# Zeros on TensorE inside the scans, the second expert's list on VectorE, and an early Silu table

## The chip, the cores and the metric

The kernel runs on one core of a Trainium2 chip. The time is device microseconds of that core, for the whole layer, all inputs in DRAM at the start and the output in DRAM at the end. The core has a matrix engine (TensorE, "PE" in the profile, with its weight loads as "PEld"), VectorE ("DVE"), ScalarE ("ACT"), GpSimd ("POOL") and SyncE ("SP", which issues most DMAs here). Lower is better.

## The reference

One encoder layer on 512 tokens of 1024 features, in float32. A mixer (eight heads of a chunked state-space scan beside eight heads of attention with a forget gate) is followed by a layer norm; then a mixture of 16 experts, top 2 of one group of four, and a second layer norm:

```
proj = x @ w_in + b_in                  # z, xBC, dt, q, k, v, f
xbc  = silu(causal_conv(xBC));  y = ssd_scan(...) * silu(z), group RMS norm
att  = forgetting_attention(q, k, v, log_sigmoid(f))
h    = layer_norm(alpha * x + concat(y, att) @ w_out)
...
g_idx = top1(softmax(h @ rg_w + rg_b));  e_val, e_idx = top2(softmax(h @ re_w[g_idx] + re_b))
for e in range(16):
    act = silu(h @ w_gate[e]) * (h @ w_up[e])
    out = out + combine[:, e:e+1] * (act @ w_down[e])
return layer_norm(alpha * h + out)
```

## The kernel before, in words

Products are made of two halves: each float32 operand is split into a rounded part (made by ScalarE) and a remainder (made by VectorE or GpSimd), and three products hi*hi, hi*lo, lo*hi are added in PSUM. `split` and `wsplit` make such pairs.

The first half of the kernel is the mixer. Two generators are woven into TensorE's stream: `prep(g)` makes the projections, convolutions and row forms of one scan group (g = 0, 1), and `scan(g)` runs the four chunks of its scan. `fill_stream` supplies further projections between the steps. In `prep`, `x_rows(c)` transposes chunk c of the two convolved tiles `x2[0]`, `x2[1]` into a PSUM bank `pxt`, which VectorE reads into xd and xsd. In `scan`, `decay(c)` makes the decay logits `pl` (a bank with the tag "s") and then the products of B and C in `pcb`. `pxt`, `pcb`, `pms` and others share two PSUM banks with the tag "t": a new tile waits until the last reader of the one that held its bank has finished. TensorE's order is written by hand throughout (`MANUAL`); the order of VectorE, ScalarE, GpSimd and SyncE is made by a planner with its own costs, except inside `tc.manual_schedule(engines=VECTOR)`, where the order in the code holds for VectorE, ScalarE and GpSimd. Instructions that come later in the code and outside may still be placed between these.

Such a hand-ordered section stands between the mixer and the experts (lines 1334 to 1403). It makes the output projection, the first layer norm and the routing by blocks of 128 tokens: `choose` ranks, `seat` numbers each expert's tokens in `place`, `weigh` makes the weights (`r1` is the exponential of the second choice's logit). The first expert's tokens are collected specially: a gather for two blocks, and for the other two a product with one-hot matrices (`picks`, `px_add`) into the banks `px`. `split` turns px into `xgh` and `xgl`, the first expert's input.

Each other expert needs a list. `seats_of` compares `seats` (1 to 128 along a row) with a token's place and makes four one-hot matrices of 128x128, on the engine that it is given; `list_of` multiplies them on TensorE with `entry` (token number and weight), and VectorE makes the index `ix` and the weight `wc`; `gather` fetches the rows of `hb` (the layer norm's result in DRAM) by an indirect DMA of GpSimd. `call(e)` is all three. The expert loop (from line 1418) runs for expert e: `gate_up` in four steps; after three (`EARLY`) `call(e + 2)`; Silu and the multiplication; `xg_T` transposes the next expert's rows; `act_T` transposes the activations; `down` multiplies by w_down, one expert later. The second expert's `call(1, False)` stands after the first step of the first expert; `weights_of_first` makes the lists' weights for the first three experts inside the second expert.

Memory on the chip is given out by tags: "u" (weights and larger tiles) and "q" (small ones, 6 buffers, among them the one-hot matrices and the activations).

Of the kernel before, what the change touches and what calls it, by code (L numbers as in the profile page):

```python
# [9 lines left out]
BF16 = mybir.dt.bfloat16  # L10
# [6 lines left out]
P = 128  # L17
# [52 lines left out]
def hybrid_layer(ctx: ExitStack, tc: tile.TileContext, x, xT, wu, w16, bT, bz, bv, b16, cw, cb,  # L70
# [15 lines left out]
    def bank(tag, name):  # L86
        return ps.tile([P, 512], F32, tag=tag, name=name)
# [65 lines left out]
    def Q(name, dt=F32):  # L153
        return slab.tile([P, 256], dt, tag="q", name=name, bufs=NQ)
# [3 lines left out]
        return t_[:, :512], t_[:, 512:]  # L158


    idle = Q("idle", BF16)[:, :P]
    V.memset(idle, 0.0)
    cx = big.enter_context(tc.tile_pool(name="cx", bufs=1))
    ph1 = ExitStack()
    sm = ph1.enter_context(tc.tile_pool(name="sm", bufs=1))
# [287 lines left out]
    def prep(g):  # L453

        w = G_[g]
        u0 = 6 + 3 * g
        hs = slice(4 * g, 4 * g + 4)
        if g:
            load_unit(u0)
        r = []  # L460
        if g:
            yield from proj_T(u0, 0, r)
            load_unit(u0 + 1)
        else:
            yield from proj_T2(u0, r)
            r = [conv_in(pt, m) for m, pt in ((1, r[0]), (0, r[1]))]
            done.add("u6")
            yield 0.0
        b2 = conv2(r.pop() if g == 0 else conv_in(r.pop(), 4 * g), 4 * g)
        w["bh"], w["bl"] = halves("b")  # L470
        split_half(w["bh"], w["bl"], b2)
        if g:
            yield from proj_T(u0, 1, r)
        c2 = conv2(r.pop() if g == 0 else conv_in(r.pop(), 4 * g + 1), 4 * g + 1)
        w["ch"], w["cl"] = halves("c")
        split_half(w["ch"], w["cl"], c2)
        yield from proj_T(u0 + 1, 0, r)
        load_unit(u0 + 2)
        if g == 0:
            SY.dma_start(bz_sb, bcast_rows(bz, 512))  # L480
            SY.dma_start(g_sb, bcast_rows(ssd_g, 512))
        x2 = [conv2(conv_in(r.pop(), 4 * g + 2), 4 * g + 2)]
        pbt = bank("t", "pbt")
        for c in range(3):
            T.transpose(pbt[:, c * P:(c + 1) * P], b2[:, c * P:(c + 1) * P], identf)
        yield 0.32
        w["bth"], w["btl"] = halves("bt")
        split_half(w["bth"][:, :3 * P], w["btl"][:, :3 * P], pbt[:, :3 * P])
        yield from proj_T(u0 + 1, 1, r)
        x2.append(conv2(conv_in(r.pop(), 4 * g + 3), 4 * g + 3))  # L490
        xeh, xel = (rows4(U(n, F32R)) for n in ("xeh", "xel"))

        xd2 = [U("xd2", F32R).rearrange("p (t g d) -> p t g d", t=2, g=2) for _ in range(2)]
        xdp = [xd2[c // 2][:, c % 2] for c in range(NT)]
        xsd = rows4(U("xsd"))
        zs = rows4(U("zs"))
        w.update(xdp=xdp, xeh=xeh, xel=xel, xsd=xsd, zs=zs)

        def x_rows(c):
            pxt = bank("t", "pxt")[:, :256]  # L500
            for m in range(2):
                T.transpose(pxt[:, m * P:(m + 1) * P], x2[m][:, c * P:(c + 1) * P], identf)
            xd = Q("xd")
            tt4(xd, pxt, dth[:, c, hs], OP.mult)
            A.activation(xdp[c][:, 0], xd, AF.Copy)
            if c < 3:
                xe = Q("xe")
                tt4(xe, xd, dec[:, c, hs], OP.mult)
                A.activation(xeh[:, c], xe, AF.Copy)
            tt4(xsd[:, c], pxt, dsh[:, hs], OP.mult)  # L510
            V.tensor_tensor(xdp[c][:, 1], xd, xdp[c][:, 0].bitcast(F32), op=OP.subtract)
            if c < 3:
                V.tensor_tensor(xel[:, c], xe, xeh[:, c].bitcast(F32), op=OP.subtract)

        for t in range(NT):
            yield from proj_R(u0 + 2, t, r)
            zf = Q("zf")
            V.tensor_tensor(zf, r.pop(), bz_sb[:, g * 256:(g + 1) * 256], op=OP.add)
            th = Q("zth")
            A.activation(th, zf, AF.Tanh, scale=0.5)  # L520
            V.scalar_tensor_tensor(zs[:, t], th, 1.0, zf, op0=OP.add, op1=OP.mult)
            if t >= XLAG[g]:
                x_rows(t - XLAG[g])
                yield 0.22
        for t in range(NT - XLAG[g], NT):
            x_rows(t)
            yield 0.22

    def scan(g):
# [9 lines left out]
        def decay(c):  # L539

            cs = slice(c * P, (c + 1) * P)
            pl = bank("s", "pl")
            for i in range(2):
                T.matmul(pl, lhsT=csel[:, c], rhs=RL[g][i], start=(i == 0), stop=False)
            T.matmul(pl, lhsT=identb, rhs=maskl[:, None, :].to_broadcast([P, 4, P]), start=False, stop=True)
            pcb = bank("t", "pcb")[:, :P]
            for i, (b_, c_) in enumerate((("bh", "ch"), ("bh", "cl"), ("bl", "ch"))):
                T.matmul(pcb, lhsT=w[b_][:, cs], rhs=w[c_][:, cs], start=(i == 0), stop=(i == 2))
            lt = U("lt")[:, :512].rearrange("p (h l) -> p h l", l=P)
            V.tensor_tensor(lt, pl.rearrange("p (h l) -> p h l", l=P),  # L550
                            ac3[:, c, hs][:, :, None].to_broadcast([P, 4, P]), op=OP.subtract)
            A.activation(lt, lt, AF.Exp)
            V.tensor_tensor(lt, lt, pcb[:, None, :].to_broadcast([P, 4, P]), op=OP.mult)
            mt[c] = [h_.rearrange("p (h l) -> p h l", l=P) for h_ in halves("mt")]
            split(*mt[c], lt)
# [321 lines left out]
    if MANUAL:  # L877
        ctx.enter_context(tc.manual_schedule(engines=MANUAL))
    g_sb, bz_sb = halves("g_bz", F32)
    pt = bank("t", "idle")  # L880
    for _ in range(10):
        T.matmul(pt, lhsT=idle, rhs=idle[:, None, :].to_broadcast([P, 4, P]), start=True, stop=True)
    first = prep(0)
    until("u6", first)
    weave(gates(), f=first)
# [79 lines left out]
    def entry_of(e):  # L965
        return lambda t: entry[:, t, EO[e]]

    def call(e, weights=True):
        se = seats_of(lp, lambda t: place[:, t, EO[e]:EO[e] + 1], G)
        ix, wc = list_of(lp, se, entry_of(e), weights=weights)  # L970
        gather(ix, xgs[e % 2])
        lists[e] = [ix, wc if weights else se]
# [325 lines left out]
    def weigh():  # L1298
# [8 lines left out]
        for k in (1, 0):  # L1307
            V.scalar_tensor_tensor(oh[k], CH["rank"][:, :, 1:5], float(k), og, op0=OP.is_equal, op1=OP.mult)
            if k:
                t_ = R([4, 4], "t_")  # L1310
                V.tensor_tensor(t_, oh[k], lg4[:, :, 1:5], op=OP.mult)
                oh0, oh1 = (o_.rearrange("p t g e -> p t (g e)") for o_ in oh)
                V.tensor_reduce(r1, t_.rearrange("p t g e -> p t (g e)"), axis=AX.X, op=OP.add)
                A.activation(r1, r1, AF.Exp)
        yield
        V.tensor_reduce(gs, gx, axis=AX.X, op=OP.add)
        V.scalar_tensor_tensor(gs, r1, 1.0, gs, op0=OP.add, op1=OP.mult)
# [16 lines left out]
    with tc.manual_schedule(engines=VECTOR):  # L1334
# [54 lines left out]
            picks(t)  # L1389
        norm_bias(3)  # L1390
        norm_store(3, hb, G)
        px_add(hh[2], pick[2], range(KC))
        dsp[0, 2] = wsplit(raw[0, 2])
        wg = weigh()
# [2 lines left out]
        for hf in range(2):  # L1397
            px_add(hh[3], pick[3], range(4 * hf, 4 * hf + 4), True)
            split(*(t_[:, hf * 4:hf * 4 + 4] for t_ in xt_), px[hf].rearrange("p (k s) -> p k s", s=P))
        for t in range(2, 4):  # L1400
            norm_store(t, ub, G)
        load_pieces(NPRE, NPRE + GATED, G)
# [1 line left out]

    def weights_of_first():

        lists[0] = list_of(lp, seats_of(lp, lambda t: place[:, t, EO[0]:EO[0] + 1], G), entry_of(0))
        for e in (1, 2):
            lists[e][1] = list_of(lp, lists[e][1], entry_of(e), tokens=False)[1]

        pn = bank("s", "pcnt")[:, :16]
        for tt in range(NT):
            T.matmul(pn, lhsT=onesb, rhs=mskb[:, tt], start=(tt == 0), stop=(tt == NT - 1))
        V.tensor_reduce(cnt_i, pn, axis=AX.X, op=OP.max)
        rt.close()

    at = {}
    for e in range(NEXP - 2):
        load_pieces(NPRE + 12 * e + (0 if e else GATED), NPRE + 12 + 12 * e)
        gu = gate_up(e, xt_, "pj" if e else "o")  # L1420
        for n in range(EARLY):
            next(gu)
            if e == 0 and n == 0:
                call(1, False)
        call(e + 2, bool(e))
        if e == 0:
            drop(wg)
        if e == 1:
            weights_of_first()
        drop(gu)  # L1430
        xt_ = xg_T(xgs[(e + 1) % 2])
        for d in DOWN[e]:
            def between(f):
                if f == ACT_AT and d != e and e in DOWN[e]:
                    at[e] = act_T(e)
            finish(d, down(d, at.pop(d), between=between))
        if e not in DOWN[e]:
            at[e] = act_T(e)
# [182 lines left out]
```

## Time and profile before

| | us |
|---|---|
| median of 3 runs (lowest, highest) | 629.06 (626.08, 634.25) |
| profiled execution, its own time | 632.85 |
| its span, first to last instruction | 631.1 |
| TensorE busy | 578.6 (92%) |
| VectorE busy | 526.4 (83%) |
| ScalarE busy | 409.7 (65%) |
| GpSimd busy | 195.8 (31%) |
| mean granted clock of TensorE | 0.973 |

Times in the profile are microseconds from the span's start. "PEclk" is the clock that TensorE was granted, as a share of 2.4 GHz. Line numbers are those of the kernel before.

### The profile page before, as it was taken

The page shows a single profiled execution, that of the slowest core. Times are in us where ns is not written, and L with a number is a line of the kernel's source. Part 1 is how long each engine was busy: PE and PEld are TensorE (multiplying, and loading weights), DVE is VectorE, ACT ScalarE, POOL GpSimd, SP SyncE. Part 2 cuts the span into 40 slices and gives each one's busy share as a digit, 9 for nine tenths or more (in the row PEclk, how much of TensorE's full clock was granted, in tenths as well). Part 3 has the DMA queues.
Part 4 walks back from the last instruction along what each step waited for, and adds up shares of the span by engine and source line. Part 5 has one row for each costly group of instructions (what it writes and reads, how often), then busy time and mean ns, then how long its engine had stood idle before and what let it go on. Part 6 is the DMA issues. An engine that isn't in the chain of part 4 may idle for free.

```text
span 631.1 us, 9108 instructions
## 1 busy us (share of the span) xinstructions
PE 578.6 (92%) x3020; PEld 472.7 (75%) x3021; DVE 526.4 (83%) x904; ACT 409.7 (65%) x640; POOL 195.8 (31%) x221
## 2 busy tenths in 40 slices
PE   6997997899999989999789999999999999999790
PEld 4786887788777758778667888888888888877550
DVE  3897598888668787668778999999999999999883
ACT  5575363543577776422267888888888888888660
POOL 6300000033553441014472223433343233412341
PEclk9998898999999999999889999999999999999996
DMA  8621021221222174994799999999999999998531
GB/s 264 209 68 60 8 77 59 84 68 65 70 68 66 36 238 133 389 344 175 281 389 319 304 382 344 386 361 358 355 346 342 328 352 373 346 339 287 190 122 61
DMA packets 62102, 142.73 MB, mean 226 GB/s; under 512 B 10073, under 2 KB 10073, under 8 KB 62048
## 3 DMA queue, kind: packets, MB, share of 16 engines
q1 hardware_dynamic: 55712, 127.88, 56.4%
q0 software_dynamic: 6336, 14.20, 7.6%
q8 instruction: 25, 0.41, 0.3%
q14 instruction: 29, 0.24, 0.1%
HBM read 136.26 MB, written 14.68 MB: 239 GB/s over the span
## 4 chain that ended last, share of the span: by engine, by line
PE 52%; DVE 16%; DMA 16%; issue 7%; ACT 6%; POOL 2%; POOLq 0%; SPq 0%; ACTq 0%; DVEq 0%
DMA xg<-ub,ix 6%; PE pw L807 4%; PE pg L1004 4%; PE pg L1006 4%; PE pg L1005 4%; PE pjT L241 4%; PE pu L1004 4%; PE pu L1006 4%; PE pu L1005 4%; PE py L1043 3%; PE py L1041 3%; PE py L1042 3%; DMA ub<-yo,ix 3%; PE pjR L265 3%; DMA xg<-hb,ix 2%
## 5 line engine op out<-in xcount | busy, mean ns | idle before, releaser
L987 ACT ACTIVATE eh<-wf 128x1024 fp32r<-128x1024 f32 x188 | 198.7, 1060 | 49.6 <-PE pg L1006 16.4
L1004 PE MATMUL pg<-eh,xgh 128*128 128x512 f32 x128 | 53.3, 416 | 0.8 <-ACT xgh L90 0.8
L958 POOL DMA_INDIRECT xg<-hb,ix x16 | 21.5, 1343 | 99.9 <-PE pg L1006 77.6
L1006 PE MATMUL pg<-eh,xgl 128*128 128x512 f32 x128 | 50.2, 393 | 1.3 <-DVE xgl L91 1.3
L1049 POOL DMA_INDIRECT ub<-yo,ix x14 | 27.2, 1945 | 74.5 <-ACT at L90 57.7
L937 POOL TENSOR_SCALAR se<-seats,place 128x128 bf16<-128x128 f32 x64 | 49.5, 784 | 1.6 <-PE pat L1022 1.1
L1004 PE MATMUL pu<-eh,xgh 128*128 128x512 f32 x128 | 49.9, 390 | 0.0
L1006 PE MATMUL pu<-eh,xgl 128*128 128x512 f32 x128 | 49.8, 389 | 0.0
L1041 PE MATMUL py<-eh,at 128*128 128x512 f32 x120 | 48.5, 404 | 1.0 <-ACT at L90 0.7
L241 PE MATMUL pjT<-xh,wh 128*128 128x512 f32 x112 | 47.6, 425 | 1.6 <-DVE kl L671 1.6
L1043 PE MATMUL py<-eh,at 128*128 128x512 f32 x120 | 47.1, 392 | 0.0
L241 PE MATMUL pjT<-xh,wl 128*128 128x512 f32 x112 | 45.0, 402 | 0.0
L241 PE MATMUL pjT<-xl,wh 128*128 128x512 f32 x112 | 45.0, 402 | 0.0
L265 PE MATMUL pjR<-wh,xh 128*128 128x256 f32 x128 | 38.6, 302 | 1.2 <-DVE vf L643 1.2
L265 PE MATMUL pjR<-wl,xh 128*128 128x256 f32 x128 | 37.5, 293 | 0.0
L265 PE MATMUL pjR<-wh,xl 128*128 128x256 f32 x128 | 37.4, 292 | 0.0
L130 POOL TENSOR_TENSOR rst<-rst,mhalf 128x1 f32<-128x1 f32 x8 | 4.6, 578 | 100.5 <-DVE rst L129 100.5
L1006 PEld LDWEIGHTS pg<-eh,xgl 128*128 128x128 f32 x128 | 24.1, 188 | 7.4 <-DVE xgl L91 2.2
L225 POOL TENSOR_TENSOR wl<-wr,wh 128x512 fp32r<-128x512 f32 x16 | 21.4, 1362 | 25.9 <-ACT wh L220 25.9
L1004 PEld LDWEIGHTS pg<-eh,xgh 128*128 128x128 f32 x128 | 24.2, 189 | 5.3 <-ACT xgh L90 1.2
L220 ACT ACTIVATE wh<-wr 128x1024 fp32r<-128x1024 f32 x22 | 23.1, 1054 | 7.5 <-PE pjT L241 3.4
L1006 PEld LDWEIGHTS pu<-eh,xgl 128*128 128x128 f32 x128 | 24.0, 188 | 5.1
(971 smaller groups left out, 1756.4 us busy)
## 6 DMA issues: line engine op xcount, KB each, us to landing
wf<-in_w_up SPq DMA_DIRECT2D x64, 512.0 KB
wf<-in_w_gate SPq DMA_DIRECT2D x64, 512.0 KB
wf<-in_w_down SPq DMA_DIRECT2D x62, 512.0 KB
wr<-in_wu SPq DMA_DIRECT2D x22, 512.0 KB
wor<-in_w_out SPq DMA_DIRECT2D x8, 512.0 KB
hh<-in_x SPq DMA_DIRECT2D x4, 512.0 KB
hb<-hh POOLq DMA_DIRECT2D x4, 512.0 KB, 4.8
ub<-hh POOLq DMA_DIRECT2D x4, 512.0 KB, 5.6
```

What stands on the lines that cost most here:

```text
L220: A.activation(h_, wr_, AF.Copy)
L241: T.matmul(pt, lhsT=w_[:, k % 4, m * P:(m + 1) * P], rhs=x_[k], start=(i == 0), stop=(i == 23))
L265: T.matmul(pt, lhsT=x_[k][:, t * P:(t + 1) * P], rhs=w_[:, k % 4, :], start=(i == 0), stop=(i == 23))
L807: T.matmul(pw, lhsT=m_[k][:, ts_], rhs=wo[k][w_][:, c_], start=(i == 0), stop=(i == 11))
L937: eng.tensor_scalar(r[t], seats, place_(t), None, op0=OP.is_equal)
L987: A.activation(h_, src, AF.Copy)
L1004: T.matmul(pt, lhsT=h_[:, k], rhs=wh_[:, f], start=(k == 0), stop=False)
L1005: T.matmul(pt, lhsT=h_[:, k], rhs=wl_[:, f], start=False, stop=False)
L1006: T.matmul(pt, lhsT=l_[:, k], rhs=wh_[:, f], start=False, stop=(k == KC - 1))
L1041: T.matmul(pt, lhsT=h_[:, f], rhs=wh_[:, c_], start=(f == 0), stop=False)
L1043: T.matmul(pt, lhsT=l_[:, f], rhs=wh_[:, c_], start=False, stop=(f == 3 and rows is None))
L1049: G.indirect_dma_start(out=ub, out_offset=bass.IndirectOffsetOnAxis(ap=ix, axis=0), in_=yo, in_offset=None, bounds_check=S - 1, oob_is_err ...
```

## The change

There are three groups of edits. (1) The ten products of zeros at the start become a function `idle(pt, n)`, which multiplies zeros (a tile of one column, read 128 and 512 times) into a PSUM bank. It is called with 6 ahead of the transposes of `x_rows(0)`, in both groups, and with 7 ahead of `pcb` of the first chunk of the first group. (2) The second expert's matrices are made by VectorE in the hand-ordered section, right after the last block's layer norm has been stored, and its list and gather follow the splits of the first expert's input, ahead of that expert's products. The first expert's own matrices (for its weights) are made one expert earlier, and its list is made last in `weights_of_first`. (3) A Silu of `r1`, whose result nobody reads, follows the exponential of `r1` on ScalarE.

```diff
-    idle = Q("idle", BF16)[:, :P]
-    V.memset(idle, 0.0)
+    zeros = const.tile([P, 1], BF16, name="zeros")
+    V.memset(zeros, 0.0)
+
+    def idle(pt, n):
+
+        for _ in range(n):
+            nc.tensor.matmul(pt, lhsT=zeros.to_broadcast([P, P]), rhs=zeros.to_broadcast([P, 512]), start=True, stop=True)
...
         def x_rows(c):
-            pxt = bank("t", "pxt")[:, :256]
+            pxt = bank("t", "pxt")
+            if c == 0:
+                idle(pxt, 6)
+            pxt = pxt[:, :256]
...
-            pcb = bank("t", "pcb")[:, :P]
+            pcb = bank("t", "pcb")
+            if c == 0 and g == 0:
+                idle(pcb, 7)
+            pcb = pcb[:, :P]
...
-    pt = bank("t", "idle")
-    for _ in range(10):
-        T.matmul(pt, lhsT=idle, rhs=idle[:, None, :].to_broadcast([P, 4, P]), start=True, stop=True)
+    idle(bank("t", "idle"), 10)
...
-    def call(e, weights=True):
-        se = seats_of(lp, lambda t: place[:, t, EO[e]:EO[e] + 1], G)
+    def call(e, weights=True, se=None):
+        se = se or seats_of(lp, lambda t: place[:, t, EO[e]:EO[e] + 1], G)
...
                 A.activation(r1, r1, AF.Exp)
+
+                A.activation(R([], "tab"), r1, AF.Silu)
...
         norm_store(3, hb, G)
+        se1 = seats_of(lp, lambda t: place[:, t, EO[1]:EO[1] + 1], V)
         px_add(hh[2], pick[2], range(KC))
...
             split(*(t_[:, hf * 4:hf * 4 + 4] for t_ in xt_), px[hf].rearrange("p (k s) -> p k s", s=P))
+        call(1, False, se1)
         for t in range(2, 4):
             norm_store(t, ub, G)
...
-        lists[0] = list_of(lp, seats_of(lp, lambda t: place[:, t, EO[0]:EO[0] + 1], G), entry_of(0))
         for e in (1, 2):
             lists[e][1] = list_of(lp, lists[e][1], entry_of(e), tokens=False)[1]
+        lists[0] = list_of(lp, lists[0], entry_of(0))
...
-        for n in range(EARLY):
+        for _ in range(EARLY):
             next(gu)
-            if e == 0 and n == 0:
-                call(1, False)
         call(e + 2, bool(e))
         if e == 0:
             drop(wg)
+            lists[0] = seats_of(lp, lambda t: place[:, t, EO[0]:EO[0] + 1], G)
```

## Rows read from the trace of the kernel before

**Rows 1.** Stretches: busy time of each engine, granted clock, DMA share, GB/s.
```profile
core 0: us, PE busy (x) PEld busy (x) DVE busy (x) ACT busy (x) POOL busy (x), PEclk, DMA share, GB/s
6.40:9.30 2.90, 2.90 (x14) 2.21 (x12) 0.69 (x1) 1.26 (x2) 0.69 (x1) 1.00 0.99 328
...
50.30:53.70 3.40, 3.40 (x19) 3.40 (x18) 2.43 (x7) 1.22 (x4) 0.00 (x0) 0.51 0.03 5
...
61.05:67.40 6.35, 6.35 (x17) 5.09 (x18) 3.83 (x9) 2.09 (x4) 0.00 (x0) 0.50 0.27 82
...
104.90:108.30 3.40, 3.40 (x18) 3.40 (x18) 2.90 (x8) 0.00 (x0) 0.33 (x1) 0.51 0.00 0
...
196.00:200.00 4.00, 2.44 (x13) 1.59 (x11) 3.96 (x10) 1.66 (x6) 2.52 (x4) 1.00 0.37 131
...
313.10:324.10 11.00, 10.99 (x54) 8.59 (x54) 10.57 (x19) 8.31 (x10) 7.63 (x9) 1.00 1.03 382
...
327.10:330.20 3.10, 3.09 (x14) 3.00 (x15) 1.15 (x2) 1.68 (x3) 2.01 (x5) 0.50 1.04 394
...
384.00:400.00 16.00, 16.00 (x81) 13.15 (x80) 15.33 (x20) 13.74 (x17) 5.86 (x6) 1.00 1.00 345
```

**Rows 2.** Timeline of TensorE in the mixer: start, duration, line, operation, [idle before <-releaser].
```profile
2.87 3.85 PE L882 MATMUL idle<-idle 128*128 128x512 bf16 x10 [2.87 <-DVE idle L162]
...
47.24 0.27 PE L502 MATMUL pxt<-identf,acc 128*128 128x128 f32 x1
49.39 0.33 PE L502 MATMUL pxt<-identf,acc 128*128 128x128 f32 x1 [1.88 <-DVE acc L436]
...
61.05 0.87 PE L548 MATMUL pcb<-c,b 128*128 128x128 f32 x3 [2.73 <-DVE xsd L445]
...
104.44 0.33 PE L502 MATMUL pxt<-identf,acc 128*128 128x128 f32 x1 [2.31 <-DVE rst L129]
...
198.29 0.50 PE L723 MATMUL po<-pl,v 128*128 128x512 f32 x1 [1.56 <-DVE pl L91]
```

**Rows 3.** Timeline of TensorE around the first two experts; last line from the chain.
```profile
312.01 0.50 PE L1004 MATMUL pg<-eh,xgh 128*128 128x512 f32 x1 [0.55 <-ACT xgh L90]
...
313.11 0.50 PE L1006 MATMUL pg<-eh,xgl 128*128 128x512 f32 x1 [0.37 <-DVE xgl L91]
...
327.11 1.97 PE L980 MATMUL pxg<-identf,xg 128*128 128x128 f32 x8 [2.85 <-DMA xg<-hb,ix]
...
329.93 0.43 PE pg L1004
```

**Rows 4.** Timeline of VectorE in the scans.
```profile
54.12 0.42 DVE L518 TENSOR_TENSOR zf<-pjR,g_bz 128x256 f32<-128x256 f32 x1 [1.28 <-PE pjR L265]
...
70.84 0.69 DVE L550 TENSOR_TENSOR lt<-pl,acum 128x512 f32<-128x512 f32 x1 [4.56 <-PE pl L545]
...
109.82 0.42 DVE L91 TENSOR_TENSOR mL<-pms,mH 128x256 fp32r<-128x256 f32 x1 [1.24 <-ACT mH L90]
```

**Rows 5.** Timelines of ScalarE and VectorE around the first expert.
```profile
291.62 0.48 DVE L1273 TENSOR_SCALAR se<-seats,place 128x128 bf16<-128x128 f32 x2
...
311.27 0.21 ACT L1314 ACTIVATE arena<-arena 128x4 f32<-128x4 f32 x1 [0.43 <-DVE arena L1313]
311.38 1.07 ACT L90 ACTIVATE xgh<-px 128x512 fp32r<-128x512 f32 x2
...
322.44 1.28 ACT L1012 ACT_TABLE_LOAD   x1
...
326.28 0.41 DVE L1016 TENSOR_TENSOR ac<-sg,pu 128x256 f32<-128x256 f32 x1
```

**Rows 6.** Timeline of GpSimd around the first expert; last line: landings of all gathers.
```profile
311.99 7.27 POOL L937 TENSOR_SCALAR se<-seats,place 128x128 bf16<-128x128 f32 x8
319.72 1.39 POOL L958 DMA_INDIRECT xg<-hb,ix  x1 [0.46 <-issue]
...
DMA to landing us min/median/max: 3.3/7.3/8.7
```

## The prediction

> **What bounds the kernel now.** I read the profile from the coarse to the fine: busy time and granted clock by stretch, then TensorE's own timeline where the clock is low, then whoever ended each wait, then that engine's queue. In the long middle TensorE is busy 16.00 us of 16 at a granted clock of 1.00 [rows 1], so whatever moves its start moves the end. What it loses lies before that, in two forms: waits, and the time after a wait in which it runs at 0.50 to 0.51, the lower of its two levels (1.2 instead of 2.4 GHz). Four waits matter: 1.88 us at 49.39 (for the second half of x2), 2.73 us at 61.05 (for xsd, the last reader of the PSUM bank that pcb takes), 2.31 us at 104.44 (the second group's x2; the view names rst, which ended at nearly the same time) [rows 2], and 2.85 us at 327.11 (the second expert's gather) [rows 3]. After each comes a stretch at the lower level: 50.30 to 53.70, 61.05 to 67.40, 104.90 to 108.30 and 327.10 to 330.20 [rows 1]. At half speed they lose 1.7, 3.2, 1.7 and 1.55 us. A shorter wait, 1.56 us at 198.29, was not followed by one [rows 1, 2]. Together: 9.8 us of waiting and 8.1 us of low clock, the most that this change can touch.
>
> **Do zeros hold the clock?** In this kernel ten of them run from 2.87 [rows 2], and the products behind them begin at 6.4 with the clock at 1.00 [rows 1]. So dense zeros count as work. One costs what a 128x512 product costs: 10.99 us for 46 products and eight tiny ones at full clock [rows 1], 0.23 us each; double that, 0.46 us, at the lower level.
>
> **The six zeros ahead of pxt, group 0.** They write the bank that the transposes then write. The first transpose ran at 47.24 without waiting [rows 2], so the zeros can start there too: 6 x 0.23 = 1.4 us inside a gap of 1.88. About 0.5 us of idleness is left, under the 1.56 that did no harm. The 1.7 us of low clock should go. VectorE takes only part: the next zf ended 1.28 us of its idleness [rows 4], and before that it is busy. So its work ahead of pcb comes 1.3 us earlier. Bounds: 0 (the clock falls all the same) to -1.7. If the cover were gone the zeros would cost their 1.4 us. **Value: -1.3.**
>
> **The seven zeros ahead of pcb.** This is the place I doubt. They write pcb, and pcb's bank is what TensorE waits for at 61.05; the first zero inherits that wait. So they run behind it, not in it: 7 x 0.46 = 3.2 us at the lower level, 1.6 us at the higher. TensorE is on the path here (VectorE idles 4.56 us until pl, which stands behind the projections [rows 4]), so nothing covers them. What they may give back: this low stretch lasted 6.35 us, the other three 3.1 to 3.4 [rows 1]. If solid zeros at its head cut it to 3.4, 3.2 of these pass under zeros and 0.1 is lost after them: 3.3 in all against the 3.2 that the long stretch loses now. Bounds: -1.6 (zeros at full clock and no low stretch) to +3.2 (zeros as pure addition). **Value: 0.**
>
> **The six zeros ahead of pxt, group 1.** The same as in group 0, in a gap of 2.31 us. They leave 0.9 us idle. Behind the low stretch VectorE idles 1.24 us at 109.82 [rows 4], in a chain that TensorE's transposes begin, and then it is the bound for some microseconds. Bounds 0 to -1.7, **value -1.2.** The scans: -2.5.
>
> **The second expert's matrices and list.** GpSimd now makes the eight matrices of two experts from 311.99 to 319.26, and the gather goes out at 319.72 [rows 6]. It lands about 7.3 us later. In the change four VectorE instructions of 0.24 us (two took 0.48 us [rows 5]) stand behind norm_bias(3) and ahead of the weight remainder and of weigh(): everything after them on VectorE is 1.0 us later. TensorE's four list products move into the wait ahead of the first expert, for nothing, and save some 0.2 us between its products. The two small VectorE steps that give the index stand behind both xgl remainders, so the gather goes out near 316.2 and lands at 323.5, or 324.9 with the longest landing of 8.7 us [rows 6]. On GpSimd's queue the gather is now ahead of two stores of ub and two loads of w_down; these can be 5 to 6 us late, which costs nothing as long as their readers come tens of microseconds later (ub's first adder behind the second expert, the w_down pieces one expert further on).
>
> **Silu's table.** It goes from 322.44, where it takes 1.28 us ahead of the first Silu, to right behind the exponential of r1 at 311.27 [rows 5]. ScalarE's order is by hand there, and next in its queue is xgh, for which TensorE waits (312.01 [rows 3]). So r1 is ready 1.0 us later, then come 1.28 us for the table and 0.2 us for the small Silu; xgh, which began at about 311.45, begins at 313.9. The first product goes to 314.4; the first one that needs xgl, at 313.11 [rows 3], goes to 315.1, +2.0, since xgl no longer has to wait for VectorE.
>
> Beside this, a rule of the Trainium skill (ScalarE: Activation LUTs, What ACT_TABLE_LOAD costs): a switch of sets costs the load of about 1283 ns and a drain of about 1380 ns, 2.66 us in all. The trace agrees on the load (1.28 us) but shows no drain: the load starts within 0.02 us of the ScalarE instruction ahead of it. By the page the first products would be an estimated 1.4 us later still, and my total with them.
>
> **The sum at the second expert.** From 313.11 to 324.1 TensorE is without a gap, so +2.0 - 0.2 = +1.8 goes through to the end of the first expert's products: 325.9. Ahead of them it now idles from 311.6 to 314.4, 2.8 us, and every wait of 1.88 us or more above was followed by low clock: +1.6, so 327.5. The gather has landed. The eight transposes follow at once (0.9 us at full clock), but the second expert's products stand behind the transposes of the first one's activations, whose second half ends at 326.69, 2.4 us after TensorE's last product (327.11 less 2.85) [rows 3, 5]; a weight remainder sits between the halves on VectorE and I see nothing that moves it. With 0.3 us of transposes: 327.5 + 2.7 = 330.2, against 329.93 now [rows 3] plus 0.1 for the rest of its low clock. D = +0.2, called 0. So the wait of 2.85 us goes, and its time returns as 1.8 us ahead of the first expert, a low stretch there, and a wait for activations that the gather used to cover. Bounds: -4.9 (no delay of xgh and no low stretch: 324.1 - 0.2 + 0.9 + 0.3 = 325.1) to +3.2 (two low stretches, one of them 6.35 us long). **Value: 0.**
>
> **The other edits** have one answer. The first expert's matrices move one expert earlier on GpSimd, whose work there has slack; a zero tile of one column is filled instead of 128; the lists' order in weights_of_first only permutes small products. If the third expert's matrices come late behind the gather, TensorE waits some 0.5 us at its list; that is in the range.
>
> **Rivals.**
> *Forecast:* scans -2.5, experts 0. The profiled execution took 632.85 us: 630.4 by its own sum. The median of the three runs is 629.06, 3.8 below it. 629.06 - 2.5 = 626.6; a faster execution probably has less low clock to give back, so I say 627.0. Chance 0.45.
> *The gather's wait goes whole:* if xgh does not stand behind the table (the r1 chain done before px) or activations come sooner, D is -4.9 and the time 629.06 - 7.4 = 621.7. For it: 2.85 us of plain wait and 1.55 of low clock. Against: the hand-written ScalarE order. Chance 0.22.
> *ScalarE makes the first expert late and the clock falls twice:* D = +3.2; with -2.5, 629.8. It decides from the point where xgh starts later than about 314. Chance 0.15.
> *The slow one, zeros that do not do what they say:* the clock falls after 49.4 and 104.4 all the same and pcb's zeros are pure addition, since they stand behind the wait for its bank. Place: 61; price 3.2 with no gain at pxt; 629.06 + 3.2 = 632.3. For it: pcb's releaser is a reader of its own bank. Against: the ten zeros at the start. It decides if the low clock behind pcb lasts 6 us after the zeros. Chance 0.18.
>
> **How the numbers follow.** The likeliest case is 627.0. The three runs of before spread over 8.2 us, so each case has some 3 us of its own. From 621.0 to 633.0 leaves out the better half of the second case and the upper tail of the last. Two per cent are 12.6 us, about what a measurement of this kernel can tell from no change; only if all bounds on one side met, with a run to match, would it show: faster 0.03, within 0.95, slower 0.02.
>
> **What would show it.** Right: the clock near 1.00 after both pxt waits; zeros at pcb directly behind xsd and not before; xgh at about 314 with the table load ahead of it; the second expert's transposes with no DMA wait, and a wait for activations behind them. Wrong: xgh still near 311.5, zeros before xsd's end, or a planner that, with the zeros in its account, puts VectorE's work of the scans in another order, whose cost I can't see from here.

## The result, and the profile after

The changed kernel takes 633.80 us (median of 19 executions, 628.82 to 640.19) where the kernel before, on the same chip, takes 629.05 (19 executions, 622.07 to 634.25). The ratio is 1.0093, 95% interval 1.0065 to 1.0122: slower by about 6 us. A second comparison (below) gave 1.0106 (1.0068 to 1.0144). I had forecast 627.0 in a range of 621 to 633.

The two profiled executions alone tell the opposite. After's took 630.73 us (span 629.0, mean granted clock 0.976), one of its faster ones; before's 632.85, one of its slower ones. So a comparison of these two traces shows what changed in the order of the work, and not what it costs on the average. Eighteen more traces, one from each run below, are needed for that.

Stretches of the changed kernel, with the columns of [rows 1]:

```profile
50.80:53.00 2.20, 2.20 (x21) 2.20 (x21) 2.12 (x7) 1.19 (x4) 0.00 (x0) 1.00 0.03 7
60.40:63.60 3.20, 3.20 (x10) 1.83 (x9) 2.08 (x7) 1.26 (x3) 0.00 (x0) 0.52 0.45 151
103.80:106.60 2.80, 2.80 (x26) 2.80 (x24) 2.26 (x7) 0.00 (x0) 0.43 (x1) 1.00 0.00 0
106.60:110.60 4.00, 0.24 (x3) 0.01 (x1) 3.33 (x11) 1.89 (x6) 0.55 (x1) 1.00 0.00 0
111.30:114.70 3.40, 3.40 (x19) 3.40 (x18) 2.09 (x7) 2.02 (x5) 0.00 (x0) 0.50 0.00 0
...
312.80:316.10 3.30, 3.30 (x9) 2.56 (x8) 2.38 (x4) 1.06 (x1) 2.31 (x3) 0.50 0.14 52
340.00:343.40 3.40, 3.40 (x10) 2.66 (x9) 0.55 (x1) 1.33 (x2) 2.35 (x4) 0.50 1.06 390
```

The clock now stays at 1.00 behind both pxt places (50.80, 103.80), where it was 0.51 [rows 1]. It is at the lower level at pcb (60.40), as before but for half as long, and at new places: 111.30, 312.80 and 340.00 (and 285.4 to 288.8, ahead of the experts, for which no run here isolates a reason). What TensorE waited for ahead of 60.40 and 111.30 stands in its timeline of the scans:

```profile
47.69 1.48 PE L167 MATMUL pxt<-zeros 128*128 128x512 bf16 x6
...
49.01 0.27 PE L511 MATMUL pxt<-identf,acc 128*128 128x128 f32 x1
49.85 0.33 PE L511 MATMUL pxt<-identf,acc 128*128 128x128 f32 x1 [0.58 <-DVE acc L442]
...
59.90 3.02 PE L167 MATMUL pcb<-zeros 128*128 128x512 bf16 x7 [2.64 <-DVE xsd L451]
62.36 1.09 PE L560 MATMUL pcb<-c,b 128*128 128x128 f32 x3
...
100.84 1.48 PE L167 MATMUL pxt<-zeros 128*128 128x512 bf16 x6
...
103.44 0.33 PE L511 MATMUL pxt<-identf,acc 128*128 128x128 f32 x1 [1.00 <-DVE rst L129]
...
110.66 0.41 PE L511 MATMUL pxt<-identf,acc 128*128 128x128 f32 x2 [3.82 <-DVE xsd L451]
```

The zeros ahead of pxt fill their waits: 1.88 us became 0.58, 2.31 became 1.00 [rows 2]. Those ahead of pcb stand behind their wait of 2.64 us and run for 3.02 us, most of it at half clock; the products of B and C follow at 62.36. And 7 us behind the second group's transposes there is a wait of 3.82 us that the kernel before does not have: there it was four of 0.62 to 1.22 us (TensorE of the kernel before):

```profile
110.30 0.44 PE L502 MATMUL pxt<-identf,acc 128*128 128x128 f32 x2 [0.93 <-DVE mL L91]
...
112.91 0.44 PE L560 MATMUL pms<-identf,zs 128*128 128x128 f32 x2 [0.75 <-DVE xsd L445]
...
115.99 0.41 PE L502 MATMUL pxt<-identf,acc 128*128 128x128 f32 x2 [1.22 <-DVE xsd L445]
...
117.02 0.44 PE L502 MATMUL pxt<-identf,acc 128*128 128x128 f32 x2 [0.62 <-DVE mL L91]
```

VectorE's timeline of the changed kernel shows why (columns as in [rows 4]):

```profile
110.10 0.42 DVE L451 TENSOR_TENSOR xsd<-pxt,dsh 128x256 f32<-128x256 f32 x1
110.44 0.41 DVE L522 TENSOR_TENSOR xel<-xe,xeh 128x256 fp32r<-128x256 f32 x1
110.77 0.42 DVE L91 TENSOR_TENSOR mL<-pms,mH 128x256 fp32r<-128x256 f32 x1
```

The planner, which makes VectorE's order here, has put mL behind xsd and xel; in the kernel before it came at 109.82 [rows 4], ahead of the steps that lead to xsd, and released the next pxt after 0.93 us of waiting. Now the next pxt is released by xsd, at the end of that chain. Around the first two experts, TensorE (columns as in [rows 3]):

```profile
310.98 0.50 PE L1014 MATMUL pg<-eh,xgh 128*128 128x512 f32 x1 [2.87 <-ACT xgh L90]
...
312.21 0.50 PE L1016 MATMUL pg<-eh,xgl 128*128 128x512 f32 x1 [0.51 <-DVE xgl L91]
...
324.63 1.03 PE L990 MATMUL pxg<-identf,xg 128*128 128x128 f32 x8
326.42 0.44 PE L1032 MATMUL pat<-identf,ac 128*128 128x128 f32 x2 [0.76 <-DVE ac L1026]
327.89 0.44 PE L1032 MATMUL pat<-identf,ac 128*128 128x128 f32 x2 [1.03 <-DVE ac L1026]
...
337.71 0.42 PE L955 MATMUL plist<-entry,se 128*128 128x3 bf16 x8 [0.99 <-DVE wc L964]
339.10 0.24 PE L1427 MATMUL pcnt<-mskb,onesb 128*128 128x16 bf16 x4 [0.96 <-DVE wc L964]
```

and ScalarE:

```profile
308.72 0.20 ACT L1324 ACTIVATE arena<-arena 128x4 f32<-128x4 f32 x1 [0.54 <-DVE arena L1323]
308.94 1.28 ACT L1326 ACT_TABLE_LOAD   x1
310.23 0.21 ACT L1326 ACTIVATE arena<-arena 128x4 f32<-128x4 f32 x1
310.35 1.07 ACT L90 ACTIVATE xgh<-px 128x512 fp32r<-128x512 f32 x2
```

xgh stands behind the table load, TensorE waits 2.87 us for it, the clock falls (312.80), the second expert's gather (sent at 313.78) is waited for by nobody, and two waits for activations follow the transposes. The second wait in `weights_of_first` (0.96 us at 339.10, the first expert's list now last, behind its VectorE step) is new, and so is the low clock behind it. By windows of 1 us (length times one minus the granted clock), the low clock of the first 350 us cost 10.2 us in this trace and 11.9 in before's: six stretches in each, at other places.

### The profile page after: what moved, and what is told of

Its sections match the earlier page's. It is cut to its first block, busy times and chain, and to the rows that moved or that the text cites. A ratio compares the mean times of both kernels' runs of the same rounds, so it can differ in the third digit from the quotient of the medians.

```text
span 629.0 us, 9150 instructions
## 1 busy us (share of the span) xinstructions
PE 580.7 (92%) x3040; PEld 472.2 (75%) x3040; DVE 527.5 (84%) x908; ACT 410.2 (65%) x641; POOL 189.5 (30%) x217
## 4 chain that ended last, share of the span: by engine, by line
PE 57%; DVE 16%; DMA 12%; issue 7%; ACT 6%; POOL 1%; POOLq 0%; SPq 0%; ACTq 0%; DVEq 0%
PE pw L819 7%; DMA xg<-ub,ix 6%; PE pg L1014 4%; PE pg L1016 4%; PE pg L1015 4%; PE pu L1014 4%; PE pu L1015 4%; PE pu L1016 4%; PE py L1053 3%; PE py L1051 3%; PE py L1052 3%; PE pjT L247 3%; PE pjR L271 3%; DMA ub<-yo,ix 3%; DVE acc L439 2%
## 5 line engine op out<-in xcount | busy, mean ns | idle before, releaser
L947 POOL TENSOR_SCALAR se<-seats,place 128x128 bf16<-128x128 f32 x60 | 44.7, 755 | 2.0 <-PE pat L1032 1.4
L271 PE MATMUL pjR<-wh,xh 128*128 128x256 f32 x128 | 37.9, 296 | 1.2 <-DVE vf L655 1.2
L1014 PEld LDWEIGHTS pu<-eh,xgh 128*128 128x128 f32 x128 | 24.6, 192 | 5.3
```

The source lines that it names most:

```text
L271: T.matmul(pt, lhsT=x_[k][:, t * P:(t + 1) * P], rhs=w_[:, k % 4, :], start=(i == 0), stop=(i == 23))
L947: eng.tensor_scalar(r[t], seats, place_(t), None, op0=OP.is_equal)
L1014: T.matmul(pt, lhsT=h_[:, k], rhs=wh_[:, f], start=(k == 0), stop=False)
```

## The experiments

Each run was timed in five rounds against the kernel before on the same chip; a ratio is followed by its 95% interval. Each diff is against the kernel before and leaves out the start's zeros, which every kernel takes from the new column, unless it says "against the changed kernel".

**The three groups of edits, alone.** The zeros:

```diff
             pxt = bank("t", "pxt")
+            if c == 0:
+                idle(pxt, 6)
...
             pcb = bank("t", "pcb")
+            if c == 0 and g == 0:
+                idle(pcb, 7)
```

> The zeros at the start from a column, and the zeros ahead of pxt (twice) and of pcb; the second expert's list, the Silu table and the order of the lists as before. Theory 1 (the loss is at the experts): TensorE's x2 waits shrink as in the trace after (1.88 to 0.58 us), so 0 to 2.5 us faster than before. Theory 2 (the zeros lose it: those ahead of pcb only add, and the new order of VectorE's work makes the 4.0 us wait after the second group's transposes): 3 to 6 us slower, as the whole change is.

Measured 1.0012 (0.9973 to 1.0052): 0.8 us slower, between the two theories, with an interval (-1.7 to +3.3 us) that reaches into both. The list, its engine and the order in `weights_of_first`:

```diff
+        se1 = seats_of(lp, lambda t: place[:, t, EO[1]:EO[1] + 1], V)
...
+        call(1, False, se1)
...
         for e in (1, 2):
             lists[e][1] = list_of(lp, lists[e][1], entry_of(e), tokens=False)[1]
+        lists[0] = list_of(lp, lists[0], entry_of(0))
```

> The second expert's list early (its matrices by VectorE, its gather ahead of the first products) and the new order in weights_of_first; no zeros in the scans, no early Silu table. Theory 1, first form (the order in weights_of_first): the wait for pxg's gather goes (2.85 and 1.6 us of low clock), the second wait of 0.96 us with 1.6 us of low clock comes, and VectorE's matrices cost about 1: between 3 us faster and 1 us slower. Theory 1, second form (the early gather itself, or its matrices, harm more than this trace shows): 3 to 6 us slower. Theory 2: 1 to 4 us faster.

Measured 0.9982 (0.9947 to 1.0018): no harm alone, against theory 1's second form. The table:

```diff
                 A.activation(r1, r1, AF.Exp)
+                A.activation(R([], "tab"), r1, AF.Silu)
```

> Only the tiny Silu behind r1's Exp (and the zeros at the start from a column). Its table load of 1.28 us stands ahead of xgh on ScalarE, and the load that stood later among the first expert's products goes. Theory 1 with the table as its cause: xgh 1.5 us later, the first products with it, and a stretch at the low clock behind that: 2 to 4 us slower. Theory 1 without it, and theory 2: within 1.5 us of before.

Measured 1.0009 (0.9977 to 1.0042). And only the start:

```diff
-    idle = Q("idle", BF16)[:, :P]
-    V.memset(idle, 0.0)
+    zeros = const.tile([P, 1], BF16, name="zeros")
+    V.memset(zeros, 0.0)
```

> Only the zeros at the start come from a column held in const in place of a tile of the Q pool; nothing else is changed. All theories: within 1 us of before. If it is 3 us or more slower, the tile given back to the pool, by the order that the scheduler makes of it, is the cause, and neither theory holds.

Measured 0.9987 (0.9953 to 1.0020). Four times no change that its interval shows, where the whole loses 1%: either the whole was mismeasured, or parts harm each other.

**The whole again, and the pairs.** The changed kernel as it is:

> The changed kernel once more. The parts alone gave ratios to the kernel before of 1.0012 (zeros), 0.9982 (list), 1.0009 (table) and 0.9987 (start alone): if parts add up, the whole is within 0.3% of before, 626 to 630 us (theory 3: the first comparison of the whole was off by its scatter). If two parts harm each other (theory 4), it is 4 to 7 us slower again, as at first.

Measured 1.0106 (1.0068 to 1.0144): theory 3 falls. Then the changed kernel without the zeros in the scans (against the changed kernel):

```diff
-            if c == 0:
-                idle(pxt, 6)
...
-            if c == 0 and g == 0:
-                idle(pcb, 7)
```

> List and table early, no zeros in the scans. Theory 4, list with table: VectorE's matrices for the second expert stand ahead of r1, so r1's Exp, the table load and xgh follow each other on the path (the first products waited 2.87 us for xgh with both, 1.36 with the list alone, 0.55 or nothing without the list): 2 to 4 us slower than the list alone, thus 629 to 632, and most of the whole's loss. Theory 3: within 1.5 us of before.

Measured 1.0008 (0.9979 to 1.0037). The trace shows the wait of 2.88 us for xgh, but the time is that of before (within -1.3 to +2.3 us): list and table together are not the loss. Without the table (against the changed kernel):

```diff
-                A.activation(R([], "tab"), r1, AF.Silu)
```

> Zeros and list, no early table. Theory 4, list with table: as the list and the zeros alone, 626 to 630 us. If the zeros and the list harm each other instead (the clock falling at places where the zeros moved the work to): 631 to 635.

Measured 1.0059 (1.0024 to 1.0094). Without the early list (the lines of the second diff above taken back, against the changed kernel):

```diff
-        call(1, False, se1)
...
+            if e == 0 and n == 0:
+                call(1, False)
```

> Zeros and early table; the second expert's list as before. Theory 4, list with table: as zeros and table alone, 627 to 631 us. If zeros and table harm each other: 631 to 635.

Measured 1.0049 (1.0014 to 1.0084). With these each group is there and not there in four pairs. The zeros cost 0.0041, 0.0077, 0.0040 and 0.0092 (with the means of the two runs of the zeros, one of which follows, and of the whole), on the average 0.62% or 3.9 us; the table 0.28% or 1.7 us; the list 0.19% or 1.2 us. With ratios good to 0.0035, such an average is good to 0.0025 or 1.6 us. The zeros are most of the loss, the table probably a part, the list unproven; theory 4, list with table, falls. Theory 2 stands as to the place, though the zeros alone lose less than it said.

**Which zeros?** Two places taken out of the whole, against the changed kernel:

```diff
-            if c == 0 and g == 0:
-                idle(pcb, 7)
```

> The whole change without the seven zeros ahead of pcb. By now the zeros as a group are worth about +3.8 us (mean of the four pairs with and without them). Theory 5, the zeros ahead of pcb are an addition with nothing behind it (1.4 us in the traces whose clock stays up, and 1.7 more where the clock falls on them): 1.5 to 3 us faster than the whole (which stood 5.0 above before), so 2 to 3.5 above before. If they earn their time: as the whole or slower.

Measured 1.0100 (1.0048 to 1.0153), from six executions: no gain, a miss for theory 5.

```diff
-            if c == 0:
+            if c == 0 and g == 0:
                 idle(pxt, 6)
```

> The whole change without the six zeros ahead of the second group's pxt. With these, VectorE gets mL behind xsd and xel, and TensorE's four waits of 0.62 to 1.22 us become one of 3.82, followed by a stretch at the low clock in five traces of five. Theory 6, that order is the loss: the four short waits come back, and 1.5 to 3 us are gained against the whole, so 2 to 3.5 above before. If the order is harmless: within 1 us of the whole, or slower, since the wait of 2.31 us comes back.

Measured 1.0074 (1.0043 to 1.0105); the four short waits came back as expected, and 1.2 to 2 us were perhaps gained against the whole's two ratios. The pcb place alone:

```diff
             pcb = bank("t", "pcb")
+            if c == 0 and g == 0:
+                idle(pcb, 7)
```

> Only the seven zeros ahead of pcb (and the start's zeros from a column). Theory 5: 1.5 to 3 us slower than before. My prediction's value for this step: 0, bounds -1.6 and +3.2.

Measured 1.0080 (1.0049 to 1.0112), 5 us: theory 5, and beyond its price. A first attempt at a better version, with the old order in `weights_of_first`:

```diff
+            if c == 0 and g == 0:
+                idle(pxt, 6)
...
+        se1 = seats_of(lp, lambda t: place[:, t, EO[1]:EO[1] + 1], V)
...
+        call(1, False, se1)
```

> A version put together from what the runs so far say is harmless: zeros ahead of the first group's pxt alone, the second expert's list early, the old order in weights_of_first, no table. The list alone took 1.8 us less from px to the second expert's lists in the traces, and gave 2.1 back behind them (the second wait of 0.96 us in weights_of_first and the low clock after it); with the old order that is not given back. Theories 5 and 6: 2 to 4 us faster than before, 624 to 626. If the order in weights_of_first is not the cause: within 1 us of before.

Measured 1.0002 (0.9968 to 1.0036), a miss. The second wait in `weights_of_first` is gone as intended. (In the trace of the list alone the wait was there, but not the low clock that I had put behind it.) TensorE there, first with the list alone, then in this kernel:

```profile
333.88 0.42 PE L951 MATMUL plist<-entry,se 128*128 128x3 bf16 x8 [1.00 <-DVE wc L960]
335.27 0.24 PE L1421 MATMUL pcnt<-mskb,onesb 128*128 128x16 bf16 x4 [0.96 <-DVE wc L960]
```

```profile
337.55 0.51 PE L953 MATMUL plist<-entry,se 128*128 128x3 bf16 x8 [1.00 <-DVE wc L962]
338.05 0.24 PE L1423 MATMUL pcnt<-mskb,onesb 128*128 128x16 bf16 x4
```

**What was still open.** The zeros again, and the whole without those ahead of pcb again:

> The zeros alone once more (as in the first experiment, 1.0012). The seven ahead of pcb alone gave 1.008. Theory 5 (those ahead of pcb cost, those ahead of pxt change little): 2.5 to 5 us slower than before, and the first comparison was low by scatter. Theory 7 (the zeros ahead of pxt earn back what those ahead of pcb cost): within 1.5 us of before again.

Measured 1.0043 (1.0007 to 1.0079).

> The whole without the zeros ahead of pcb once more (1.0100 from six executions). Theory 5: 1.5 to 3 us above before (ratio 1.0025 to 1.005), and the first comparison was high by scatter. If it stays at 1.008 to 1.012, the zeros ahead of pcb cost nothing inside the whole, and the zeros ahead of pxt with list and table are its loss.

Measured 1.0103 (1.0047 to 1.0159), again from six executions. So the first was no scatter: inside the whole, taking the pcb zeros out gains nothing. The zeros of one group of pxt, first the second group:

```diff
+            if c == 0 and g == 1:
+                idle(pxt, 6)
```

> Only the six zeros ahead of the second group's pxt. Theory 6 (the order they give VectorE: one wait of 3.82 us always followed by the low clock, for four short ones): 0.5 to 2 us slower than before. My prediction's value for the step: -1.2, bounds 0 and -1.7.

Measured 1.0092 (1.0057 to 1.0126): more than theory 6's price. Its trace has the wait, and the clock behind it, at half for 5.5 us:

```profile
108.19 0.66 PE L511 MATMUL pxt<-identf,acc 128*128 128x128 f32 x2 [3.81 <-DVE xsd L451]
```

```profile
108.19:113.70 5.51, 5.51 (x27) 5.51 (x28) 3.68 (x10) 2.36 (x5) 0.00 (x0) 0.52 0.00 0
```

```diff
+            if c == 0 and g == 0:
+                idle(pxt, 6)
```

> Only the six zeros ahead of the first group's pxt. The wait of 1.87 us there was followed by the low clock in the kernels without these zeros in three traces of five, so its gain should be three fifths of 1.7, 1 us (0 to 2 us faster than before). My prediction's value for the step: -1.3.

Measured 0.9969 (0.9925 to 1.0013): on the side of a gain, not proven. Last, the seven zeros of pcb moved from behind the wait into it:

```diff
             pl = bank("s", "pl")
+            if c == 0 and g == 0:
+                idle(pl, 7)
```

> The seven zeros moved ahead of the first pl, whose products waited for nothing: so they run inside the wait for xsd and not behind it (no other zeros but the start's, no list, no table). The wait of 2.73 us ahead of pcb should shrink by 7 x 0.23 = 1.6 to about 1.1, and pcb should start when it did. Theory 5 (ahead of pcb the zeros lost because they stood behind the wait): within 1.5 us of before, or up to 1.5 faster. If these zeros harm wherever they stand (the clock): 3 to 5 us slower, as the 1.008 of those ahead of pcb.

Measured 1.0005 (0.9969 to 1.0042). TensorE with the zeros ahead of pcb alone, and then ahead of pl alone:

```profile
59.96 3.00 PE L167 MATMUL pcb<-zeros 128*128 128x512 bf16 x7 [2.64 <-DVE xsd L451]
62.40 1.10 PE L558 MATMUL pcb<-c,b 128*128 128x128 f32 x3
```

```profile
55.26 1.69 PE L167 MATMUL pl<-zeros 128*128 128x512 bf16 x7
...
58.86 0.52 PE L558 MATMUL pcb<-c,b 128*128 128x128 f32 x3 [1.22 <-DVE xsd L451]
```

The same zeros now run for 1.69 us ahead of the wait, which shrinks from 2.73 to 1.22 us; pcb's products start at xsd's end and in this trace run at full clock (0.52 us for the three, not 1.10), and the loss of 0.8% is gone. So with no other change beside them, these zeros lose by where they stand, and not wherever they stand. With the first group's pxt:

```diff
+            if c == 0 and g == 0:
+                idle(pxt, 6)
...
             pl = bank("s", "pl")
+            if c == 0 and g == 0:
+                idle(pl, 7)
```

> Zeros ahead of the first group's pxt and ahead of the first pl, nothing else: the version that the runs point to. The first alone gave 0.9969 (0.9925 to 1.0013). With the second in the wait: 1 to 3 us faster than before, 624.5 to 626.5. If zeros ahead of pl harm: 2 to 4 us slower than before.

Measured 0.9950 (0.9914 to 0.9986), median 623.97 us: faster than both kernels.

## Why the prediction was wrong

In short, the step that failed is the zeros ahead of pcb, valued 0: alone they cost 5 us, of which 1.4 are seen at their place as plain addition. Two orders that were put at nothing cost more in the traces: that of VectorE's work behind the second group's zeros (0.9 us net at the place) and that of the lists (2.3 us). How these make the 6 us of the whole is not shown in full, as the last part of this section says.

**I read one execution's low clock as the kernel's.** In the trace of before each of the four waits was followed by half clock, and I booked that as recoverable. A nearly identical kernel (only the start's zeros changed) ran the same waits in the scans without any. Its TensorE and two of its stretches:

```profile
49.73 0.33 PE L509 MATMUL pxt<-identf,acc 128*128 128x128 f32 x1 [1.87 <-DVE acc L442]
...
59.88 0.52 PE L556 MATMUL pcb<-c,b 128*128 128x128 f32 x3 [2.73 <-DVE xsd L451]
```

```profile
50.06:53.40 3.34, 3.34 (x30) 3.34 (x30) 2.65 (x8) 1.80 (x6) 0.00 (x0) 1.00 0.02 5
59.90:65.50 5.60, 5.60 (x26) 4.69 (x27) 3.81 (x9) 2.10 (x4) 0.00 (x0) 1.00 0.29 97
```

Over all 20 traces (before, after and the 18 runs), the place, the wait that TensorE had there, and in how many traces half clock followed:

```
place                          wait, us      followed by half clock in
pxt group 0, without zeros     1.86-1.88      3 of  8
pxt group 0, with zeros        0.53-0.58      0 of 12
pcb, without zeros             2.73           4 of 10 (three of them 6 us long or more)
pcb, zeros behind the wait     2.64           5 of  8
pcb, zeros ahead of pl         1.21-1.22      0 of  2
pxt group 1, without zeros     2.31-2.32      9 of 11
pxt group 1, with zeros        0.99-1.00      0 of  9
next waits, group 1, without   0.6-1.2        2 of 11
next wait, group 1, with       3.81-3.83      9 of  9 (four of them 6 us long or more)
```

So zeros inside a wait do hold the clock at that wait, which was my premise. What a filled wait gives back is then, as an estimate, the loss of one stretch, 1.7 us, times its frequency.

**Zeros ahead of pxt, group 0: value -1.3.** Mechanism right: 1.88 us to 0.58, clock at 1.00. The size was taken for certain and comes in 3 of 8 traces; alone 0.9969, 2 us faster or nothing.

**Zeros ahead of pcb: value 0, bounds -1.6 to +3.2.** This term failed. The place was right (behind the wait, as the text said). Wrong was the step "if solid zeros at its head cut it to 3.4, 3.2 of these pass under zeros". The cut itself is borne out: with these zeros none of the 5 falls is long, without them 3 of 4. But the step credits the zeros with a long stretch that 7 traces of 10 do not have, and there nothing stands against their time. Nine traces hold the full clock from the second half of the first group's pxt to that of the second group's. In the six without the pcb zeros this takes 50.52 to 50.56 us (in the start alone from 49.73 to 100.28); in the three with them 51.93 to 51.97 (in the second run of the whole from 49.60 to 101.57). That is 1.4 us of pure addition. Alone, they measured 5 us (3.1 to 7.0), nearly all of it above my upper bound; 1.4 of these are seen at the place, and the rest stays open.

**Zeros ahead of pxt, group 1: value -1.2.** The wait and the low clock there went as said, in all nine traces. The time came back 7 us later as one wait of 3.8 us in place of the short ones, with the clock down behind it each time. From the second group's second transposes to those of its last chunk the traces take 12.3 us without these zeros (mean of 11; 11.2 to 12.6) and 13.2 with them (mean of 9; 12.6 to 13.5). So the place itself shows +0.9 where I had -1.2; alone it measured +0.9% of the time, 5.8 us. I had named the planner's order as a thing that I couldn't see, and gave it neither a price nor a chance.

**The experts: D = 0.** The steps came as said: the table load ahead of xgh, the first products after 2.87 us of waiting (I had 2.8), half clock behind it, the gather hidden (2.3 to 3.1 us of waiting in the traces with the old list), the transposes at 324.63 and then two waits for activations. From the first transposes of `px` to the first product the traces take 7.31 us in the five with the old list whose clock is full there, and 9.71 to 9.72 in the four with list and table: +2.4, the shift that I had. The total is not 0 in the traces. In the same nine, the third expert's transposes follow those of `px` after 37.9 to 38.4 us with the old list and 42.3 to 42.4 with list and table, 4.2 more; first the start alone, then the changed kernel:

```profile
295.49 2.03 PE L1297 MATMUL px<-identf,xg 128*128 128x128 f32 x16
...
318.16 1.97 PE L986 MATMUL pxg<-identf,xg 128*128 128x128 f32 x8 [3.09 <-DMA xg<-hb,ix]
...
333.90 1.03 PE L986 MATMUL pxg<-identf,xg 128*128 128x128 f32 x8
```

```profile
301.27 2.03 PE L1301 MATMUL px<-identf,xg 128*128 128x128 f32 x16
...
343.62 1.03 PE L990 MATMUL pxg<-identf,xg 128*128 128x128 f32 x8
```

About 1.9 of the 4.2 are there at the second expert's first product; the trace that I had started from had half clock just ahead of the first expert (303.0 to 306.4), which made its 329.93 late. The rest, 2.3 us, comes with the new order of the lists: "only permutes small products" was wrong. The wait of 0.96 us ahead of pcnt was there in all eight traces with the new order, half clock behind it in seven, and neither in the one trace with the early list and the old order. No comparison of times isolated this order, and the times do not show the 4.2: list and table together measure 1.0008, -1.3 to +2.3 us.

The load of the table again shows no drain in the trace: Silu began 0.01 us after its end. The Trainium skill (ScalarE: Activation LUTs, What ACT_TABLE_LOAD costs) adds 1380 ns for one; no run here shows that.

**The rivals.** The slow one named pcb and pure addition. Its time of 632.3, at a chance of 0.18, is near what was found, but by luck: the clock held behind both pxt places, no fall at pcb lasted 6 us with the zeros there, and the addition seen is 1.4 us and not 3.2. It missed group 1 and the lists' order.

**How much is the clock?** Each timed execution has a span and a mean granted clock. Span times (1 - clock) estimates what was lost to the lower level, and too high: in the 20 traces 4.5 to 6.4 us of it lie behind TensorE's last product, where it has nothing left to do. In before's trace that product ends at 616.35 and the end of the span looks like this:

```profile
620.40:631.10 10.70, 0.00 (x0) 0.00 (x0) 1.28 (x1) 0.00 (x0) 1.35 (x2) 0.50 0.17 67
```

Even so it sorts the executions of before: one of 622.0 us had 0.990, one of 630.4 had 0.972, an estimated 6.2 and 17.6 us, and over the 149 executions that the comparisons list the correlation of time and estimate is 0.93. Means over the executions compared, the kernel's first and before's of the same comparison second:

```
kernel                      time, us          estimated loss to the clock, us
whole (second comparison)   633.3   627.2     15.4   12.8
pcb zeros alone             631.6   627.1     16.8   12.3
pxt group 1 alone           632.2   627.6     17.7   13.2
all zeros (both runs)       629.7   627.5     13.8   13.1
list and table              628.8   627.2     13.9   12.8
zeros ahead of pl alone     627.2   627.3     13.1   12.8
pxt group 0 and pl          624.3   627.3     11.4   12.8
```

By this estimate the losses of pcb alone and of group 1 alone are nearly all clock, 4.5 us of 4.5 and of 4.6; of the whole's 6.1 it is 2.6. But the part behind the last product differs by up to 1.9 us from trace to trace, so differences between rows are uncertain by something like that; for pcb alone, 1.4 us of plain addition should be left over, and nothing is.

**A wait that I did not book.** In before's trace TensorE also waits for the first expert's gather, and half clock stands beside it from 303.0 to 306.4. In the trace of the first group's pxt alone the same wait is longer:

```profile
303.29 3.50 PE L1291 MATMUL px<-identf,xg 128*128 128x128 f32 x16 [1.71 <-DMA xg<-hb,ix]
```

```profile
299.24 3.79 PE L1299 MATMUL px<-identf,xg 128*128 128x128 f32 x16 [4.28 <-DMA xg<-hb,ix]
```

Seven traces of the 20 have it, 1.6 to 4.3 us long. There the gather landed 6.9 to 10.0 us after it was sent, in the others (where the trace has the landing) after 5.0 to 5.9. In all seven the clock fell beside it, six times for 6.8 us or more; of the other 13, three had such a fall ahead of the first expert. So one place that no edit of the change touches moves an execution by as much as the whole change costs (an estimated 7.7 us in the trace of 4.28: the wait and half of a fall of 6.8). The two traces of the changed kernel do not have the wait. Whether a change elsewhere makes it come more often can't be told from one trace of each run, and it is a rival to the clock wherever a loss is not found at its place.

**What stays open.** The parts do not add up. Alone, the zeros of pcb and of group 1 cost 0.8 and 0.9%; both together, with those of group 0 beside them, 0.1 and 0.4% in two runs; and inside the whole the removal of the one gains nothing and of the other 0.2 to 0.3%. That a shift at one place decides whether a later wait meets half clock, or a late gather, is a way in which places so far apart could act on each other, but that is argued and not shown. Nor do the traces of the two single places show their whole loss: they took 627.18 and 626.30 us, each the fastest of its kernel's executions. In the traces, 1.4 us at pcb, 0.9 behind the second group's pxt and 4.2 at the experts, less an estimated 0.6 at the first group's pxt (1.7 times 3 of 8), come to the 6 us measured for the whole, yet the kernel with list and table and no zeros, which has the 4.2 in its trace (an execution of 632.51 us, where its median is 628.03), measured as before. So the zeros as a group are shown to make most of the loss (0.62% on the average of four pairs); by which path is not.

## What to carry to other kernels

Before booking a low clock as a gain, look at the same wait in several executions: what can be won is one stretch times how often it comes. Look there too for waits that come in some executions only, like the late gather. Filler must stand ahead of the semaphore that is waited for, so write it into a bank that is free already; in the awaited bank it is work added behind the wait. And where a planner orders another engine, filler enters its account, so compare that engine's order before and after; to a changed order belong a price and a chance.

## What the hardware showed

The same instructions with the same waits (1.9, 2.3 and 2.7 us) ran at full clock in one trace and at half in another, in kernels that differ only elsewhere. The Trainium skill (TensorE: Matmul & The Clock Gate, Part 1) says as much of a kernel's start, where one kernel measured 6, 11 or 14 products at half rate; the rows here show it in the middle of a kernel too. Over the executions of the kernel before, which spread over 12 us, time and mean clock go together (correlation 0.93 with the estimated loss). Beside falls of about 3.4 us there are long ones: behind the waits of 2.73 and 3.8 us, 7 of 13 falls lasted 6 us or more, with TensorE busy for most of that time (5.51 of 5.51 us at 108.19 above). And the first expert's gather landed 5.0 us after it was sent in one trace (the start alone) and 10.0 in another (the first group's pxt alone).
